# The last two gate blocks tile by tile, output weights in half rows, the output projection's first two token blocks together

## The chip, the cores and the metric

The kernel runs on one core of one Trainium2 chip. The metric is the device time of one execution in microseconds (us); the time of before is the median of three runs. The engines are named as in the profile: PE (TensorE, matmuls), PEld (its weight loads), DVE (VectorE), ACT (ScalarE), POOL (GpSimd) and SP (SyncE, which here issues all DMA transfers). "PSUM" is the memory that matmuls write, "bank" one of its [128, 512] float32 tiles.

## The reference, cut to what matters

One layer of a mixer over 2048 tokens of width 1024: a modulated norm, one input projection, four branches (RG-LRU, short convolution, Fourier, SSD), each gated, and one output projection of their 4 x 512 = 2048 columns.

```python
y_rg, rg_st = rglru(rg_x, lp, rg_h0, True)
y_ssd, ssd_st = ssd_branch(ssd_xbc, ssd_dt, ssd_z, lp, ssd_h0, True)
y_sc = shortconv_branch(sc_b, sc_c, sc_x, lp, rows)
y_fn = fourier_branch(fn_x)
ycat = jnp.concatenate([y_rg * jax.nn.silu(rg_g), y_sc * jax.nn.silu(sc_g),
                        y_fn * jax.nn.silu(fn_g), y_ssd], axis=-1)
return ycat.astype(h.dtype) @ lp['w_out'], rg_st, ssd_st
...
x = x + gate * out
...
return rmsnorm(x, final_norm_w)
```

## The kernel before

Every product is made of three matmuls, since an operand is kept as a high part and a rest (`split`, L210: ACT copies the high part, L139, and DVE or POOL subtracts it, L214): high by high, high by rest, rest by high. One tile of an input projection (`proj`, L229) is 8 steps of 128 rows, so 24 matmuls of 128x128 by 128x512 (L142 to L144). A block of weights (`wload`, L219) covers 128 columns; its halves come through one buffer `wraw`, and the block lies in one of two slots, `whi`/`wlo` 0 and 1, which a block frees with its last matmul.

The stages stand in the source in this order: modulation, RG-LRU, z and dt, SSD inputs, Fourier mixing, the SSD's first chunks, short convolution and RG-LRU gates, the last gate (`fngate`, four blocks of 128 columns, each over four tiles of 512 tokens), and the output projection over 16 blocks of 128 tokens. The tile framework's scheduler settles the order of each engine's instructions from its own model of times before the program runs; on the chip each queue then runs in that order, so an instruction that waits holds all behind it.

The SSD goes by 16 chunks of 128 tokens. `ssd_head` (L965) makes scores (PE L982, masked on DVE L986), the next state (L678), two products with the entering state (PE L1004, L1005, from `hs` that DVE makes in L1002), and the decayed scores `ma` (DVE L1022, L1027, L1032, L1033, with ACT and POOL). `ssd_tail` (L1037) multiplies them (L1044), gates, norms (the last step is DVE L1057), transposes (PE L1060), and stores the result by a DMA to `ycat`. `ssd_chunk(c)` is the head of chunk c+1 and the tail of chunk c. `NEARLY` chunks stand ahead of the gates; the others stand in the output projection's loop, chunk b + `NEARLY` ahead of block b.

The output projection of a token block takes four quarters of its 2048 rows (`oproj`, L1148), in the order of the branches: quarter 3 is the SSD's. A quarter is loaded from `ycat` (`oyr`), split (`ysplit`, to `oyhl`), and multiplied with the two halves of 512 columns: 24 matmuls (L1153 to L1155) into two banks, `ps_mm` and `ps_tr`. Of either there are two buffers. The 16 weight rows-of-128 are loaded in the last gate block as [128, 1024] tiles (`wo_raw`: two buffers and a weight slot that is not in use), split, and put where the tokens' columns `h_hi`, `h_lo` of a 512-token tile have been read for the last time: quarter q takes the places of tile q. The first token block's projection (`op0`) directly follows the last gate, since the gates' weight slots give it its buffers.

Of the kernel before, what the change touches and what calls it, by code (L numbers as in the profile page):

```python
# [8 lines left out]
F32 = mybir.dt.float32  # L9
# [24 lines left out]
def constants():  # L34
# [5 lines left out]
    # channel transform: [cos 0..64 | sin 0..63], with the ortho norm and the gate's half  # L40
# [6 lines left out]
    # token transform: rows in blocks (window of 256, parity)  # L47
# [10 lines left out]
    # [par*4+w][cos/sin][128][f] -> split f into two tiles  # L58
# [11 lines left out]
def layout(x, c, ctx, c_ctx, ada_w, ada_b, norm_w, w_in, w_out, rg_conv_w, rg_conv_b, rg_gate_a_w, rg_gate_a_b,  # L70
# [7 lines left out]
    # [block of columns k][row within 128][rows / 128][shift | scale]  # L78
# [43 lines left out]
def build(tc, A, out):  # L122
# [23 lines left out]
    def softplus(pl, x, n, dst, scale_in=1.0, tag=None, bufs=None):  # L146
        """dst = log(1 + exp(scale_in * x)) for a [128, n] tile, exact also where it is small."""
# [27 lines left out]
    def mbank(four):  # L175
        """a bank for a projection; with four, of those of the transposes too"""
        nbank[0] += 1
        return bank("tr" if four and nbank[0] % 2 else "mm")
# [7 lines left out]
    # ---------------------------------------------------------------- constants  # L186
# [20 lines left out]
    # ---------------------------------------------------------------- weight blocks  # L207
# [3 lines left out]
    def split(hi, lo, raw, eng):  # L211
        """raw (float32) as a high part and a rest, both of 12 bits"""
        copy_hi(hi, raw)
        eng.tensor_tensor(lo, raw, f32(hi), SUB)  # L214
# [20 lines left out]
    # ---------------------------------------------------------------- adaLN shift and scale  # L235
# [10 lines left out]
    def norm_rows(xt):  # L246
        """scales the rows of xt [128, 1024] by 1/rms"""
# [8 lines left out]
    # high and low part of the four columns side by side: one pass over the matrix' high part serves both  # L256
# [7 lines left out]
    # [k][:, who] = shift, norm_w * (1 + scale)  # L264
# [31 lines left out]
    # ---------------------------------------------------------------- normed, modulated, transposed tokens  # L296
# [30 lines left out]
    def conv_silu(pl, b, projs, n, emit, nb=3):  # L327
        """causal-ish convolution of 4 taps and silu over consecutive tiles of n tokens, each then given to emit"""
# [48 lines left out]
    # ---------------------------------------------------------------- first columns: RG-LRU input, context  # L377
# [30 lines left out]
    # the first tile of tokens and three blocks of weights run along with the columns of the modulation's matrix  # L408
# [35 lines left out]
    # dt of the context, by columns  # L444
# [45 lines left out]
    # ---------------------------------------------------------------- RG-LRU  # L490
# [788 lines left out]
```

## Time and profile before

| | |
|---|---|
| median of three runs | 1653.36 us (1651.04 to 1655.83) |
| span of the profiled execution | 1656.3 us |
| mean granted TensorE clock | 0.980 |
| busy: PE, DVE, ACT, POOL | 1569.4, 1053.3, 714.9, 564.3 us |
| gate blocks 2 and 3 | 1149.0 to 1202.5 us of the span |
| output projection | from 1202.5 us on |
| its regular period for one token block | 27.4 us |

The profiled execution has no other time than its span; it lies 2.9 us above the median and 0.5 us above the highest of the three runs. The share of busy time says which engine has the most work; where time is lost is told by the idle times in front of PE's instructions, each with the engine that ended it. A shown duration of a matmul is longer than the distance to the next one, since matmuls are pipelined: distances of starts tell the rate.

### The profile page before, as it was taken

What the parts mean: (1) busy time and instruction counts of PE and PEld (TensorE: products, weight loads), DVE (VectorE), ACT (ScalarE), POOL (GpSimd) and SP (SyncE); (2) the same over time, 40 slices, a digit from 0 to 9 for tenths busy, and PEclk for the clock granted to TensorE, in tenths of its full rate; (3) what the DMA queues carried; (4) which work ended last, traced back from release to release, by engine and by line L of the source; (5) the groups of instructions that cost most, each with busy time, mean ns of one, the idle gap of its engine ahead of it and who ended that gap; (6) DMA issues with size and microseconds to landing.
All of it is one profiled execution on the core that took longest, in us unless ns stands there. A gap on an engine that the chain in (4) does not pass through costs nothing. (4 is left out here: it accounts for less than half of the span.)

```text
span 1656.3 us, 22749 instructions
## 1 busy us (share of the span) xinstructions
PE 1569.4 (95%) x7906; PEld 1271.5 (77%) x7906; DVE 1053.3 (64%) x1837; ACT 714.9 (43%) x1383; POOL 564.3 (34%) x536
## 2 busy tenths in 40 slices
PE   6899999899899999899999999898988999999998
PEld 3687899777788778666788888785766777777787
DVE  7765354698986657644168653437468777878653
ACT  5654046557465536211222324424345544545432
POOL 5533123312211422343315345334423424243310
PEclk9999999999999999999999999999999999999999
DMA  8424232323332231454222236657575655555532
GB/s 328 153 87 135 87 99 92 106 90 104 124 116 71 83 121 58 148 156 128 77 79 61 87 109 179 174 161 233 165 254 171 183 146 171 146 170 148 162 105 70
DMA packets 182257, 220.93 MB, mean 133 GB/s; under 512 B 20183, under 2 KB 118905, under 8 KB 182142
## 3 DMA queue, kind: packets, MB, share of 16 engines
q1 hardware_dynamic: 182142, 219.48, 42.8%
q8 instruction: 62, 1.02, 0.3%
q14 instruction: 53, 0.43, 0.1%
HBM read 155.40 MB, written 64.03 MB: 132 GB/s over the span
## 5 line engine op out<-in xcount | busy, mean ns | idle before, releaser
L142 PE MATMUL ps_mm<-h_hi,whi 128*128 128x512 f32 x696 | 276.9, 401 | 5.6 <-ACT craw L347 4.5
L143 PE MATMUL ps_mm<-h_lo,whi 128*128 128x512 f32 x696 | 278.7, 400 | 1.8 <-DVE h_lo L309 1.0
L144 PE MATMUL ps_mm<-h_hi,wlo 128*128 128x512 f32 x696 | 278.3, 400 | 0.0
L142 PEld LDWEIGHTS ps_mm<-h_hi,whi 128*128 128x128 f32 x696 | 133.1, 192 | 36.2 <-ACT craw L347 5.4
L143 PEld LDWEIGHTS ps_mm<-h_lo,whi 128*128 128x128 f32 x696 | 133.3, 192 | 31.6 <-DVE h_lo L309 2.2
L144 PEld LDWEIGHTS ps_mm<-h_hi,wlo 128*128 128x128 f32 x696 | 133.6, 192 | 28.9 <-issue 1.4
L142 PE MATMUL ps_tr<-h_hi,whi 128*128 128x512 f32 x384 | 151.6, 395 | 0.0
L143 PE MATMUL ps_tr<-h_lo,whi 128*128 128x512 f32 x384 | 151.5, 395 | 0.0
L144 PE MATMUL ps_tr<-h_hi,wlo 128*128 128x512 f32 x384 | 151.1, 394 | 0.0
L1153 PE MATMUL ps_mm<-wo_hi,oyhl 128*128 128x512 f32 (+1 forms) x272 | 106.9, 393 | 7.5 <-ACT oyhl L139 7.5
L139 ACT ACTIVATE whi<-wraw 128x512 fp32r<-128x512 f32 (+1 forms) x77 | 49.6, 645 | 143.4 <-DMA wraw<-wblk 98.4
L1155 PE MATMUL ps_mm<-wo_hi,oyhl 128*128 128x512 f32 (+1 forms) x272 | 106.2, 391 | 2.8 <-DVE oyhl L214 2.7
L1154 PE MATMUL ps_mm<-wo_lo,oyhl 128*128 128x512 f32 (+1 forms) x272 | 106.9, 393 | 0.0
L1009 POOL TENSOR_TENSOR y<-y,e 128x256 f32<-128x256 f32 x32 | 35.6, 1114 | 195.3 <-DVE e L1008 195.3
L1154 PE MATMUL ps_tr<-wo_lo,oyhl 128*128 128x512 f32 (+1 forms) x256 | 100.4, 392 | 0.0
L1155 PE MATMUL ps_tr<-wo_hi,oyhl 128*128 128x512 f32 (+1 forms) x256 | 100.0, 390 | 0.0
L1153 PE MATMUL ps_tr<-wo_hi,oyhl 128*128 128x512 f32 (+1 forms) x256 | 99.1, 387 | 0.0
L214 POOL TENSOR_TENSOR wlo<-wraw,whi 128x512 fp32r<-128x512 f32 (+1 forms) x40 | 61.7, 1543 | 97.3 <-ACT whi L139 81.8
L142 PEld LDWEIGHTS ps_tr<-h_hi,whi 128*128 128x128 f32 x384 | 72.8, 190 | 16.8 <-issue 2.1
L143 PEld LDWEIGHTS ps_tr<-h_lo,whi 128*128 128x128 f32 x384 | 72.6, 189 | 16.4 <-issue 1.7
L144 PEld LDWEIGHTS ps_tr<-h_hi,wlo 128*128 128x128 f32 x384 | 72.6, 189 | 15.6 <-issue 1.1
L139 ACT ACTIVATE oyhl<-oyr 128x512 fp32r<-128x512 f32 x68 | 42.6, 627 | 96.2 <-PE ps_tr L1155 72.6
(365 smaller groups left out, 3847.9 us busy)
## 6 DMA issues: line engine op xcount, KB each, us to landing
wraw<-wblk SPq DMA_DIRECT2D x74, 256.0 KB, 3.0
oyr<-ycat SPq DMA_DIRECT2D x68, 256.0 KB, 3.4
ci<-cst_d SPq DMA_DIRECT2D x64, 256.0 KB, 3.5
xs<-xsb_d SPq DMA_DIRECT2D x31, 320.0 KB, 3.0
adar<-ada SPq DMA_DIRECT2D x16, 512.0 KB, 10.2
hf_d<-r_v SPq DMA_DIRECT2D x32, 256.0 KB, 2.2
ycat<-gy SPq DMA_DIRECT2D x32, 256.0 KB, 2.4
wo_raw<-wout SPq DMA_DIRECT2D x16, 512.0 KB
```

The source lines that it names most:

```text
L139: act.activation(dst, src, AF.Copy)
L142: pe.matmul(ps, wh, xh, start=start, stop=False)
L143: pe.matmul(ps, wh, xl, start=False, stop=False)
L144: pe.matmul(ps, wl, xh, start=False, stop=stop)
L214: eng.tensor_tensor(lo, raw, f32(hi), SUB)
L1009: pool.tensor_tensor(y[:, s], y[:, s], e[:, 0:256], ADD)
L1153: pe.matmul(p, yhl[:, 0, j], wo_hi[q][:, j, c0:c1], start=first and j == 0, stop=False)
L1154: pe.matmul(p, yhl[:, 0, j], wo_lo[q][:, j, c0:c1], start=False, stop=False)
L1155: pe.matmul(p, yhl[:, 1, j], wo_hi[q][:, j, c0:c1], start=False, stop=last and j == 3)
```

## The change

One more SSD chunk (head of chunk 2, tail of chunk 1) stands ahead of the gates and no longer in the loop. Gate blocks 2 and 3 both get their weights first, and their tiles go by turns: tile 0 of block 2, tile 0 of block 3, tile 1 of block 2, and so on. The output weights come as 32 half rows of [128, 512] through four buffers. The first two token blocks of the output projection run quarter by quarter side by side, on all four banks of `ps_mm` and `ps_tr`: quarters 0 and 1 with buffers in the weight slots, quarters 2 and 3 with those of the loop.

```diff
-    NEARLY = 1
+    NEARLY = 2
...
-        for j in range(3):
+        for j in range(2):
             w = wload(B_FNG + j)
             for tt in range(4):
                 fngate(w, j, tt)
-        w = wload(B_FNG + 3)
+
+        ws = [wload(B_FNG + j) for j in (2, 3)]
         free = wcount[0] % 2
         for tt in range(4):
-            fngate(w, 3, tt)
+            for j in range(2):
+                fngate(ws[j], 2 + j, tt)
...
-                if (4 * tt + j) % 3 < 2:
-                    r = qr.tile([128, 1024], F32, name="wo_raw", tag="wo_raw", bufs=2)
-                else:
-                    r = wp.tile([128, 1024], F32, name="wo_raw", tag=f"wlo{free}")
-                ld(r, A["wout"][4 * tt + j])
...
+                for c0 in (0, 512):
+                    cs = slice(c0, c0 + 512)
+                    r = qr.tile([128, 512], F32, name="wo_raw", tag="wo_raw", bufs=4)
+                    ld(r, A["wout"][4 * tt + j][:, cs])
...
-        op0 = [bank("mm"), bank("tr")]
-        for q in range(4):
-            yr = wp.tile([128, 4, 128], F32, name="oyr", tag="wraw", bufs=1)
-            yhl = wp.tile([128, 2, 4, 128], F32R, name="oyhl",
-                          tag=(f"whi{free}", f"whi{1 - free}", f"wlo{1 - free}", f"whi{free}")[q])
-            ysplit(0, q, yr, yhl)
-            oproj(yhl, q, op0, halves, q == 0, q == 3)
+
+        op0 = [[bank("mm"), bank("tr")] for _ in range(2)]
+        for q in range(2):
+            for b in range(2):
+                yr = wp.tile([128, 4, 128], F32, name="oyr", tag="wraw", bufs=1)
+                yhl = wp.tile([128, 2, 4, 128], F32R, name="oyhl", tag=f"{('whi', 'wlo')[b]}{(free + q) % 2}")
+                ysplit(b, q, yr, yhl)
+                oproj(yhl, q, op0[b], halves, q == 0, False)
...
+    qye = ExitStack()
+    qy = qye.enter_context(pool_of("qy", right))
+    for q in range(2, 4):
+        for b in range(2):
+            oproj(yhl_of(b, q), q, op0[b], halves, False, q == 3)
...
-                op_ = op0 if b == 0 else [bank("mm"), bank("tr")]
-                for q in range(4 if b else 0):
+                op_ = op0[b] if b < 2 else [bank("mm"), bank("tr")]
+                for q in range(4 if b >= 2 else 0):
```

What it does to the queues is seen at three places. The first is PE's queue at the end of gate block 2's first tile (`ps_tr_10486` before; `h_hi1` is token tile 1). Before, with what each instruction waits for:

```order
L144 MATMUL ps_tr_10486<-h_hi0_246,wlo_10475 128x512
L1060 MATMUL ps_bb_7660<-ident_66,y_7469 128x128 [waits DVE_49]
L1060 MATMUL ps_bb_7660<-ident_66,y_7469 128x128 x3
L142 MATMUL ps_mm_10518<-h_hi1_856,whi_10474 128x512
L143 MATMUL ps_mm_10518<-h_lo1_857,whi_10474 128x512
```

And after the change, where `whi_10613`, `wlo_10614` are block 3's weights and `whi_10603` block 2's:

```order
L144 MATMUL ps_tr_10625<-h_hi0_246,wlo_10604 128x512
L142 MATMUL ps_mm_10657<-h_hi0_246,whi_10613 128x512 [waits Activation_49]
L143 MATMUL ps_mm_10657<-h_lo0_247,whi_10613 128x512
L142 MATMUL ps_tr_10723<-h_hi1_856,whi_10603 128x512
L144 MATMUL ps_mm_10657<-h_hi0_246,wlo_10614 128x512 [waits Pool_49]
```

Block 3's first tile, with its weights, moved ahead of block 2's second tile; chunk 0's transposes (L1060) and chunk 2's head now stand behind it.

The second place is PE's queue at the first quarter 3 that has to wait for a chunk of its own. Before, that is in token block 1 (`wo_hi_10754` is quarter 2's weights, `wo_hi_10804` quarter 3's); this is the end of the stretch between chunk 1's transposes and quarter 3:

```order
L678 MATMUL ps_ba<-xw,xs 64x256 x2
L1154 MATMUL ps_mm<-wo_lo_10755,oyhl 128x512
L1155 MATMUL ps_mm<-wo_hi_10754,oyhl 128x512
L1153 MATMUL ps_tr<-wo_hi_10754,oyhl 128x512
L1004 MATMUL ps_ba<-hs,ch 128x512
L1005 MATMUL ps_ba<-hs,cl 128x512
L1154 MATMUL ps_tr<-wo_lo_10755,oyhl 128x512
L1155 MATMUL ps_tr<-wo_hi_10754,oyhl 128x512
L1153 MATMUL ps_mm<-wo_hi_10804,oyhl 128x512
```

After, in token block 2 (`wo_hi_10883` is quarter 2, `wo_hi_10981` quarter 3), from chunk 2's transposes on:

```order
L1060 MATMUL ps_bb<-ident,y 128x128 x4
L1044 MATMUL ps_bb<-xs,ma 128x64
L982 MATMUL ps_ba<-cct,bt 128x128
L1044 MATMUL ps_bb<-xs,ma 128x64 x6
L678 MATMUL ps_ba<-xw,xs 64x256 x2
L1044 MATMUL ps_bb<-xs,ma 128x64
L1155 MATMUL ps_mm<-wo_hi_10883,oyhl 128x512
L1153 MATMUL ps_tr<-wo_hi_10883,oyhl 128x512
L1154 MATMUL ps_tr<-wo_lo_10884,oyhl 128x512
L1155 MATMUL ps_tr<-wo_hi_10883,oyhl 128x512
L1004 MATMUL ps_ba<-hs,ch 128x512
L1153 MATMUL ps_mm<-wo_hi_10981,oyhl 128x512
```

The place moved by one token block, and four of quarter 2's matmuls lie between where sixteen lay.

The third is the SP queue at the end of the output weights. Before, with the first block's quarters 2 and 3 (`oyr_10882`, `oyr_10911`):

```order
L134 DMA oyr_10882<-ycat0_147 128x4x128
L134 DMA wo_raw_10768<-wout 128x1024
L134 DMA ycat3_150<-gy_10772 128x512
L134 DMA wo_raw_10806<-wout 128x1024
L134 DMA oyr_10911<-ycat0_147 128x4x128
L134 DMA wo_raw_10810<-wout 128x1024
L134 DMA wo_raw_10814<-wout 128x1024
L134 DMA wo_raw_10818<-wout 128x1024
```

After (`oyr_11048` and `oyr_11077` are the second block's quarter 0 and the first block's quarter 1, `oyr_11106` the second block's quarter 1):

```order
L134 DMA oyr_11048<-ycat0_147 128x4x128
L134 DMA wo_raw_10987<-wout 128x512
L134 DMA wo_raw_10991<-wout 128x512
L134 DMA wo_raw_10995<-wout 128x512
L134 DMA ycat3_150<-gy_10917 128x512
L134 DMA oyr_11077<-ycat0_147 128x4x128
L134 DMA wo_raw_10999<-wout 128x512
L134 DMA ycat3_150<-gy_10949 128x512
L134 DMA wo_raw_11003<-wout 128x512
L134 DMA wo_raw_11007<-wout 128x512
L134 DMA wo_raw_11011<-wout 128x512
L134 DMA oyr_11106<-ycat0_147 128x4x128
```

Of a token block's quarters, 2 and 3 stood among the last weights' loads; now no quarter beyond 1 does, and the second block's quarter 1 follows the last weight.

## Rows read from the trace of the kernel before

**Rows 1.** The page's first part: busy time, share of the span, instructions

```profile
PE 1569.4 (95%) x7906; PEld 1271.5 (77%) x7906; DVE 1053.3 (64%) x1837; ACT 714.9 (43%) x1383; POOL 564.3 (34%) x536
```

**Rows 2.** Waits of PE from 900 us on: total us, times, longest

```profile
PE ps_mm L1153 <- ACT oyhl L139: 7.5, 2, 6.2
PE ps_ba L982 <- DMA cct<-ct_d: 3.9, 1, 3.9
PE ps_ba L1004 <- DVE gm L986: 3.4, 2, 2.1
PE ps_mm L1155 <- DVE oyhl L214: 2.7, 2, 1.4
PE ps_ba L1004 <- DVE hs L1002: 2.4, 2, 2.2
```

**Rows 3.** Stretches: sum, busy PE, PEld, DVE, ACT, POOL, clock, DMA share, GB/s

```profile
1140.00:1160.00 20.00, 17.03 (x78) 12.20 (x77) 19.21 (x38) 9.84 (x28) 10.69 (x10) 1.00 0.70 209
1160.00:1180.00 20.00, 17.83 (x70) 13.97 (x69) 13.10 (x22) 7.86 (x17) 12.39 (x11) 0.91 0.47 150
...
1329.00:1356.40 27.40, 27.40 (x129) 21.21 (x128) 20.64 (x47) 13.40 (x33) 9.81 (x9) 1.00 0.54 156
```

**Rows 4.** Timeline of PE, gate blocks 2 and 3: start, duration, instruction, idle before

```profile
1149.02 0.39 PE L142 MATMUL ps_tr<-h_hi,whi 128*128 128x512 f32 x1
...
1154.10 0.47 PE L1004 MATMUL ps_ba<-hs,ch 128*128 128x512 f32 x1 [2.08 <-DVE gm L986]
...
1165.71 0.51 PE L1004 MATMUL ps_ba<-hs,ch 128*128 128x512 f32 x1 [2.17 <-DVE hs L1002]
...
1167.00 0.63 PE L142 MATMUL ps_mm<-h_hi,whi 128*128 128x512 f32 x1
1167.42 0.63 PE L143 MATMUL ps_mm<-h_lo,whi 128*128 128x512 f32 x1
...
1180.75 0.39 PE L142 MATMUL ps_tr<-h_hi,whi 128*128 128x512 f32 x1
```

**Rows 5.** Timeline of PE, output projection's first token block

```profile
1202.51 0.39 PE L1153 MATMUL ps_mm<-wo_hi,oyhl 128*128 128x512 f32 x1
...
1209.37 0.50 PE L1153 MATMUL ps_mm<-wo_hi,oyhl 128*128 128x512 f32 x1 [1.25 <-ACT oyhl L139]
...
1211.53 0.80 PE L1155 MATMUL ps_mm<-wo_hi,oyhl 128*128 128x512 f32 x1 [1.44 <-DVE oyhl L214]
...
1219.94 0.50 PE L1155 MATMUL ps_mm<-wo_hi,oyhl 128*128 128x512 f32 x1 [1.28 <-DVE oyhl L214]
...
1226.96 0.49 PE L982 MATMUL ps_ba<-cct,bt 64*128 64x128 f32 x2
```

**Rows 6.** The tile wo_raw: instructions, durations in ns, first and last start

```profile
L1187 DVE SCALAR_TENSOR_TENSOR wo_lo<-wo_raw,cols,wo_hi x4: 1283/1284/1286, 1222.1 to 1229.0; 128x1024 fp32r<-128x1024 f32 x4
```

**Rows 7.** Timeline of PE from chunk 1's transposes to quarter 3

```profile
1250.73 0.60 PE L1060 MATMUL ps_bb<-ident,y 128*128 128x128 f32 x4
...
1258.61 0.40 PE L1155 MATMUL ps_tr<-wo_hi,oyhl 128*128 128x512 f32 x1
1265.22 0.79 PE L1153 MATMUL ps_mm<-wo_hi,oyhl 128*128 128x512 f32 x1 [6.21 <-ACT oyhl L139]
```

**Rows 8.** Timeline of the SP queue in that stretch

```profile
1254.10 0.39 SPq L134 DMA_DIRECT2D ycat<-yt  x1
...
1258.18 0.43 SPq L134 DMA_DIRECT2D oyr<-ycat  x1
```

**Rows 9.** Timeline of ACT there

```profile
1264.54 0.63 ACT L139 ACTIVATE oyhl<-oyr 128x512 fp32r<-128x512 f32 x1 [5.18 <-DMA oyr<-ycat]
```

**Rows 10.** Timeline of DVE: the last part of gate block 3's weights

```profile
1165.69 0.69 DVE L214 TENSOR_TENSOR wlo<-wraw,whi 128x512 fp32r<-128x512 f32 x1
```

**Rows 11.** DVE by line and form, 1137 to 1167 us: busy us, mean ns

```profile
L1022 DVE TENSOR_SCALAR ci<-ci,pk 128x128 f32<-128x128 f32 x16 | 6.2, 438 | 0.2 <-DMA ci<-cst_d 0.2
L1033 DVE TENSOR_TENSOR ma<-ma,ci 128x512 f32<-128x512 f32 x3 | 3.8, 1277 | 0.0
```

**Rows 12.** The same from 1329 to 1356.4 us

```profile
L1022 DVE TENSOR_SCALAR ci<-ci,pk 128x128 f32<-128x128 f32 x8 | 1.7, 278 | 3.5 <-DMA ci<-cst_d 3.5
L1033 DVE TENSOR_TENSOR ma<-ma,ci 128x512 f32<-128x512 f32 x2 | 1.4, 680 | 0.0
```

More of the change, by code (lines that the diff above doesn't have):

```diff
@@ L1169, in build @@
                 fngate(w, j, tt)
-        w = wload(B_FNG + 3)
+        ws = [wload(B_FNG + j) for j in (2, 3)]
         free = wcount[0] % 2
         for tt in range(4):
-            fngate(w, 3, tt)
+            for j in range(2):
+                fngate(ws[j], 2 + j, tt)
             hi, lo = H16(f"wo_hi{tt}", 2 * tt, F32R, (4, 1024)), H16(f"wo_lo{tt}", 2 * tt + 1, F32R, (4, 1024))
             for j in range(4):
-                if (4 * tt + j) % 3 < 2:
-                    r = qr.tile([128, 1024], F32, name="wo_raw", tag="wo_raw", bufs=2)
-                else:
-                    r = wp.tile([128, 1024], F32, name="wo_raw", tag=f"wlo{free}")
-                ld(r, A["wout"][4 * tt + j])
-                if tt < 3:
-                    split(hi[:, j], lo[:, j], r, pool if j == 2 else dve)
-                else:
-                    nw = cols[:, C_SNW + j:C_SNW + j + 1]
-                    act.activation(hi[:, j], r, AF.Copy, scale=nw)
-                    dve.scalar_tensor_tensor(lo[:, j], r, nw, f32(hi[:, j]), MUL, SUB)
+                for c0 in (0, 512):
+                    cs = slice(c0, c0 + 512)
+                    r = qr.tile([128, 512], F32, name="wo_raw", tag="wo_raw", bufs=4)
+                    ld(r, A["wout"][4 * tt + j][:, cs])
+                    if tt < 3:
+                        split(hi[:, j, cs], lo[:, j, cs], r, pool if j == 2 else dve)
+                    else:
+                        nw = cols[:, C_SNW + j:C_SNW + j + 1]
+                        act.activation(hi[:, j, cs], r, AF.Copy, scale=nw)
+                        dve.scalar_tensor_tensor(lo[:, j, cs], r, nw, f32(hi[:, j, cs]), MUL, SUB)
@@ new lines, in build, with yhl_of @@
+        for q in range(2):
[4 more added lines that the diff above has]
+                oproj(yhl, q, op0[b], halves, q == 0, False)
+    def yhl_of(b, q):
+        yr = qy.tile([128, 4, 128], F32, name="oyr", tag="oyr", bufs=3)
+        yhl = qy.tile([128, 2, 4, 128], F32R, name="oyhl", tag="oyhl", bufs=2)
+        ysplit(b, q, yr, yhl)
+        return yhl
@@ L1197, in build @@
+    qye = ExitStack()
[3 more added lines that the diff above has]
+            oproj(yhl_of(b, q), q, op0[b], halves, False, q == 3)
     wpe.close()
-    with pool_of("qy", right) as qy, pool_of("q6", left) as q6:
+    with pool_of("q6", left) as q6:
         fnw = q6.tile([128, 1024], F32, name="fnw")
@@ L1204, in build @@
         ld(gate_b, gate_d.partition_broadcast(128))
-        def yhl_of(b, q):
-            yr = qy.tile([128, 4, 128], F32, name="oyr", tag="oyr", bufs=3)
-            yhl = qy.tile([128, 2, 4, 128], F32R, name="oyhl", tag="oyhl", bufs=2)
-            ysplit(b, q, yr, yhl)
-            return yhl
         def residual(p, xr, c0, c1, ss):
@@ L1261, in build @@
                 st(o_[:, 0:512], xr[:, 0:512])
+    qye.close()
     sdp.close()
```

## The prediction

> **What bounds the kernel now.** I read the page's busy times first, then PE's waits, then the timeline of PE around each of them. PE is busy for 95% of the span [rows 1]; DVE, next, for 64%. In the regular part of the output projection, from 1329 us on, PE is busy for the whole of each stretch of 27.4 us [rows 3], and the list of PE's waits [rows 2] has nothing that falls later than 1300 us. So PE's own work is the floor there, and an edit pays only where PE stands idle or runs at a lower rate. The change leaves the number of matmuls as it is and moves them, between about 1149 and 1300 us. The reader should see in [rows 2] which waits lie there: two on ScalarE's part of `oyhl` (7.5 us, 6.2 of it in one), two on VectorE's part (2.7), two on `gm` (3.4, the longer 2.1), two on `hs` (2.4, one of 2.2).
>
> The full rate is read where nothing waits: from 1180.75 [rows 4] to 1202.51 us [rows 5] lie four tiles of 24 matmuls, 21.76 us or 0.2267 us a matmul, 5.44 us a tile or quarter. Behind some waits the distance is 0.42 us (1167.00 to 1167.42 [rows 4]): that is the lower of TensorE's two clock levels, 1.2 instead of 2.4 GHz, and it follows a wait of 2.17 us in these rows. The granted clock of 1160 to 1180 us is 0.91 [rows 3].
>
> **Part 1: the first token blocks side by side, weights in half rows.** Before, 80 matmuls of the first block run from 1202.51 to 1226.96 us [rows 5], 24.45 us, where 80 x 0.2267 = 18.1 would do: 6.3 us are lost, 1.25 + 1.44 + 1.28 us as waits on `oyhl`, the rest as matmuls held up within their queue or at the lower level. With T for the projection's start at 1202.51, quarter 1 was needed at T + 5.4 and whole at T + 9.0 (1211.53); quarter 2 was needed at T + 10.9 and waited for until T + 17.4 (1219.94). Side by side, a quarter lasts for two blocks, 10.9 us, so quarter 1 is needed at T + 10.9 and quarter 2 at T + 21.8: both later than they were ready before. The last weights were split until 1229.0 + 1.3 = T + 27.8 [rows 6]; quarter 3 is now needed at T + 32.7. The second block's data are loaded in addition, one after another through one buffer in the weight slots, at most 5 us for load and split (5.4 us of PE's work covers each). The change also lets weights start sooner, since a token tile is read for the last time two tiles ahead of the next one, 10.9 us instead of 5.4. The 32 loads instead of 16 cost SP 16 more issues of some 0.4 us (as the loads of [rows 8]), in the cover of 43.5 us of matmuls. Thus the 6.3 us go, bounded by 3.3 (one load lands three us late) and 6.3. I take **-6.3**.
>
> **Part 2: the wait on `gm`.** Chunk 2's head no longer follows on the first block's projection; what stands there is chunk 3's head, with 19 matmuls, 4.3 us, between its scores and its first use of `hs`. The second wait on `gm`, 3.4 - 2.1 = 1.3 us [rows 2], is covered: **-1.3**, bounds -1.3 and 0.
>
> **Part 3: the wait of 6.2 us moves, it does not go.** Before, chunk 1's transposes are at 1250.73 us, the branch's result is stored from 1254.10 us [rows 8], the reload as a quarter is issued at 1258.18, lands some six us later, is split at 1264.54 [rows 9], and quarter 3 begins at 1265.22 us: a chain of 14.5 us, of which PE's own work covers 8.3, up to 1259.0 (the last matmul starts at 1258.61 [rows 7]). After the change blocks 0 and 1 have their chunks early. But in block 2 the transposes of chunk 2 stand right in front of quarter 3 again, with only 16 small matmuls of the chunk, two of its state, two of its entering state and four of quarter 2 between, about 4.8 us. Here the queue's order decides, not the time at which the data could be there. The chain could be as short as 10.0 us (the store 3.8 us and the load 3.4 us of the same tiles, and some 2.8 for ACT, the issues and the split) or as long as before: a wait of 5.2 to 9.7 us. I take 6.2 as before, nearer to the lower end, since the SP queue has less in it there than at 1254 us: **0**, bounds -1.0 and +3.5. Behind a wait as long as this the lower level follows in both kernels.
>
> **Part 4: the gate stretch.** The two blocks ran from 1149.02 to 1202.51 us, 53.5 us for 192 matmuls (43.5) and 2.7 us of chunk work: 7.3 us lost, of them 2.08 and 2.17 as waits on `gm` and `hs` [rows 4]. After the change two things differ. First, block 3's first tile needs its weights at once. They come no sooner, since they take the slot of block 1, whose last matmul is at 1149.02 us: the last part of them was made by VectorE at 1165.69 + 0.69 = 1166.4 us [rows 10], 17.4 us behind. In this time PE did 41 matmuls and some chunk work before; the new order gives it all of block 2's tile 0 and most of block 3's, and by counting rows up to the weights' last part PE is ahead of before by about **-1.4**. Secondly, chunk 2's head and chunk 1's tail come into the stretch. Their matmuls are only moved. Their VectorE work is not free: VectorE was busy for 19.21 of 20 us from 1140 us, and for 13.10 of the next 20 [rows 3]. From the weights' last part to the `hs` of chunk 2's second half it now has about 18.9 us of work if its operations last as in the regular part [rows 12], and 24.1 at the prices of this stretch (1277 ns instead of 680 for L1033, 438 instead of 278 for L1022 [rows 11]), while PE's queue has 16.1 us in between. PE waits 2.8 us by the one and 8.0 by the other, or not at all if VectorE gets ahead as in the idle third that it had behind 1160 us. I take **+2.8**, since POOL's tensor work, which stands beside the dear rows, is less behind 1166 us, and +0.7 for the lower level behind one wait in two: 3.5, bounds 0 and 11.
>
> The dear prices in [rows 11] are those of VectorE's operations with POOL at work for 10.7 of 20 us [rows 3]. The Trainium skill, "SBUF — State Buffer", section "SBUF: two separate sides", says that VectorE and GpSimd share a pair of SBUF ports, which one of them holds for a whole instruction while the other waits; it speaks against packing one more chunk among POOL's gate products, and by it the dear end holds as long as POOL is at work. The two row groups agree with it (1277 against 680 ns).
>
> **The sum** against the profiled execution: -6.3 - 1.3 + 0 - 1.4 + 3.5 = -5.5 us of 1656.3. The profiled run lies 2.9 us above the median, and the difference is the same for either: 1653.4 - 5.5 = 1647.9. A part of the loss before that I didn't price is 3.9 us on `cct` [rows 2], ahead of the change, which may come a few tenths sooner; I say 1648. Forecast alone: 1643 to 1653.
>
> **The rivals.** (A) The gate stretch takes back what the projection gives. It is the price of a chunk among the gates: the two blocks lose 7.3 us with one chunk among them; if the further chunk costs as much there, the 3.5 - 1.4 of part 4 become +7.3, and the sum is -6.3 - 1.3 + 7.3 = -0.3: 1653.1, no change. For it: VectorE at 19.21 of 20 us [rows 3]. Against: it has a third free behind 1160 us. (B) Slower: VectorE stays at the dear prices to the end of the gate blocks. Then chunk 2's `hs` comes 8.0 us late, 3 us more go at the lower level behind it, and the chain of part 3 takes its full 14.5 us (+3.5): -6.3 - 1.3 + 3.5 + 8.0 + 3.0 = +6.9, and without the -1.4 of part 4: 1660. It passes the time of before once the gates lose more than some 6 us beyond what they lose now. For it: rows 11; against: POOL's share there is not all tensor work that collides, and the regular part does as much per chunk at the lower prices. (C) Quarter 3 of block 2 doesn't wait: its chain ends within the cover, because chunk 2's result could be there long before. Then part 3 is -6.2 - 1.2 for the lower level behind it, instead of 0: the sum is -12.9, 1640.5. Against: chain and cover hang on one queue's order, and 10.0 us of chain do not fit in 4.8. (D) The tiles by turns might wait for weights throughout, so that the change doesn't do what it says: but only the first of block 3's tiles comes near to 1166.4 us, the others follow by 10.9 us, so this is inside the bounds of part 4.
>
> **How the numbers follow.** Forecast 0.53, A 0.25, B 0.12, C 0.10. The likeliest is the forecast, **1648**. A measurement of this kernel tells about 0.3% from no change, 5 us: faster means under 1648.4. The forecast's own range lies on both sides of this mark; of its 0.53 I give 0.36 to faster, since most of its bounds and the unpriced `cct` lie on that side, and 0.17 to no change. With C that is 0.46 for faster; A and the rest of the forecast make 0.42 for no change. B gives 0.12 for slower. For a range of 8 in 10 I leave out B's far half and the ends of C: 1640 to 1657.
>
> **What would show it.** In the profile after: the waits of L1153 and L1155 on `oyhl` shrink to one of 5 to 10 us, in token block 2, behind L1060; blocks 0 and 1 run 192 matmuls in 43.5 us without a gap; no wait on `gm` behind the projection's start; in the gate stretch a wait on weights or on `hs` of up to 8 us, and VectorE close to full from 1166 us on. Wrong would be: gaps among the 192 matmuls (part 1), VectorE's L1033 near 1.3 us up to the projection (then A or B), or no wait at block 2's quarter 3 (then C).

## The result

The changed kernel takes 1665.8 us (median of five runs, 1663.1 to 1670.1) against 1653.4 us (1648.3 to 1657.2): a ratio of 1.0075, 95% interval 1.0053 to 1.0097, so 12 us slower where 1648 was forecast. It also lies outside the range (1640 to 1657).

The page's first line of times, to be held against [rows 1], shows that no work was added to PE, and 11 us to VectorE:

```profile
PE 1569.2 (94%) x7906; PEld 1270.3 (76%) x7906; DVE 1064.7 (64%) x1850; ACT 714.7 (43%) x1399; POOL 558.9 (34%) x539
```

PE's waits of the changed kernel from 900 us on (in all, times, longest; before: [rows 2]):

```profile
PE ps_mm L1153 <- ACT oyhl L139: 11.2, 2, 7.0
PE ps_ba L982 <- DMA cct<-ct_d: 5.2, 1, 5.2
PE ps_ba L1004 <- DVE hs L1002: 4.4, 3, 2.5
PE ps_ba L1004 <- DVE gm L986: 3.8, 3, 1.6
PE ps_mm L1155 <- DVE oyhl L214: 3.2, 4, 1.7
```

The kinds of waits are the same; the one on ScalarE's part of `oyhl` has two long ones now. The timeline of PE (start, duration, instruction, idle time before it) says where; the second line is the last matmul of the gates, the next the first of the output projection, to be held against [rows 5] and [rows 7]:

```profile
1200.36 0.39 PE L142 MATMUL ps_mm<-h_hi,whi 128*128 128x512 f32 x1
...
1205.57 0.39 PE L144 MATMUL ps_mm<-h_hi,wlo 128*128 128x512 f32 x1
...
1212.93 0.80 PE L1153 MATMUL ps_mm<-wo_hi,oyhl 128*128 128x512 f32 x1 [6.97 <-ACT oyhl L139]
...
1280.52 0.60 PE L1060 MATMUL ps_bb<-ident,y 128*128 128x128 f32 x4
...
1289.96 0.50 PE L1153 MATMUL ps_mm<-wo_hi,oyhl 128*128 128x512 f32 x1 [4.20 <-ACT oyhl L139]
...
1424.52 0.50 PE L1155 MATMUL ps_mm<-wo_hi,oyhl 128*128 128x512 f32 x1 [1.67 <-DVE oyhl L214]
...
1428.90 0.49 PE L1004 MATMUL ps_ba<-hs,ch 128*128 128x512 f32 x1 [1.59 <-DVE gm L986]
```

The wait of 4.2 us at 1289.96 is the one that the prediction placed in block 2. That of 7 us at the projection's very first matmul, and those behind 1305 us, it did not have.

**Where the time went.** To add up small losses too, I took from each trace the distance of each PE instruction to the next and subtracted what its form takes where nothing waits: 0.2268 us for a matmul of 128x512, and for the chunk's forms 0.113 (L1044), 0.108 (L1060), 0.145 (L678), 0.36 (L1004), 0.425 (L1005), 0.207 (L982). The sums, in us, start 26 us ahead of chunk 1's first scores (L982), so that differences of the first 1110 us between executions are left out. "Gates" ends with the gates' last matmul; the token blocks are numbered as in the code, from 0. The rows below **after** are the experiments, which the next section explains one by one. Each ratio is against runs of before on the same chip.

| kernel | median us | ratio to before, 95% | gates | start, blocks 0 and 1 | block 2 | 3 to 7 | rest | sum |
|---|---|---|---|---|---|---|---|---|
| before | 1653.4 | 1 | 15.8 | 17.0 | 0.9 | 2.2 | 2.7 | 38.6 |
| before_again | 1654.8 | 0.9998 (0.9985 to 1.0011) | 17.7 | 15.8 | 0.9 | 2.2 | 3.1 | 39.8 |
| **after** | 1665.8 | 1.0075 (1.0053 to 1.0097) | 17.5 | 10.6 | 5.8 | **13.6** | 3.0 | 50.5 |
| lead_one | 1656.8 | 1.0024 (1.0014 to 1.0034) | 18.7 | 11.9 | 6.3 | 4.3 | 3.2 | 44.4 |
| near_two | 1655.6 | 1.0014 (1.0004 to 1.0025) | 21.2 | 9.1 | 2.4 | 2.6 | 2.5 | 37.9 |
| one_block | 1658.0 | 1.0035 (1.0020 to 1.0049) | 18.5 | 18.3 | 0.4 | 2.0 | 2.7 | 41.9 |
| no_turns | 1674.0 | 1.0119 (1.0101 to 1.0137) | 19.4 | 16.7 | 8.4 | 14.3 | 3.0 | 61.7 |
| no_turns_lead | 1669.0 | 1.0082 (1.0066 to 1.0098) | 18.0 | 14.4 | 8.6 | 7.3 | 2.9 | 51.2 |
| lead_one_rows | **1650.7** | **0.9976** (0.9966 to 0.9987) | 19.0 | 10.0 | 0.8 | 2.2 | 3.2 | 35.2 |
| lead_one_six | 1655.4 | 1.0007 (0.9998 to 1.0017) | 21.7 | 3.9 | 6.9 | 3.0 | 3.2 | 38.7 |
| lead_one_less | 1657.9 | 1.0018 (1.0009 to 1.0028) | 21.8 | 11.8 | 5.5 | 2.4 | 3.0 | 44.5 |
| turns_halves | 1653.6 | 0.9994 (0.9985 to 1.0004) | 17.0 | 15.8 | 0.4 | 1.7 | 3.2 | 38.1 |
| turns_rows | 1668.9 | 1.0081 (1.0067 to 1.0095) | 16.6 | 27.0 | 0.8 | 5.5 | 3.0 | 53.0 |
| halves_only | 1666.6 | 1.0075 (1.0062 to 1.0087) | 15.3 | 29.6 | 0.8 | 2.2 | 3.2 | 51.1 |
| rows_first_split | 1659.1 | 1.0027 (1.0017 to 1.0036) | 21.0 | 11.5 | 5.0 | 2.3 | 2.9 | 42.7 |
| first_own | 1664.7 | 1.0064 (1.0046 to 1.0082) | 17.6 | 15.3 | 6.5 | 2.5 | 2.6 | 44.5 |
| rows_first_pool | 1664.7 | 1.0056 (1.0043 to 1.0068) | 21.0 | 8.1 | 4.3 | 10.4 | 3.0 | 46.7 |

For the change: 50.5 - 38.6 = 11.9 us, as the ratio has it (0.0075 x 1653.4 = 12.4). The gates give +1.7, the start with the first three blocks 16.4 instead of 17.9 (-1.5), and blocks 3 to 7 give +11.4. The spans of the two profiled executions, 1664.0 and 1656.3 us, differ by only 7.7 us: in every other execution that has both numbers the time is 1.7 to 1.9 us above the span, so the profiled execution of before took about 1658 us, some 4.7 above its median and not 2.9. A column is one profiled execution, good to one or two us (before against before_again), so that of these three differences only the +11.4 is clear of the noise; with first_own the profiled execution was 6.6 us shorter than the median, so its sum says little, and of its trace only the waits are used.

### The profile page after: what moved, and what is told of

Its sections match the earlier page's. It is cut to its first block, busy times and chain, and to the rows that moved or that the text cites. A ratio compares the mean times of both kernels' runs of the same rounds, so it can differ in the third digit from the quotient of the medians.

```text
span 1664.0 us, 22814 instructions
## 1 busy us (share of the span) xinstructions
PE 1569.2 (94%) x7906; PEld 1270.3 (76%) x7906; DVE 1064.7 (64%) x1850; ACT 714.7 (43%) x1399; POOL 558.9 (34%) x539
## 5 line engine op out<-in xcount | busy, mean ns | idle before, releaser
L214 POOL TENSOR_TENSOR wlo<-wraw,whi 128x512 fp32r<-128x512 f32 (+1 forms) x40 | 61.7, 1542 | 101.0 <-ACT whi L139 85.5
L142 PEld LDWEIGHTS ps_tr<-h_hi,whi 128*128 128x128 f32 x384 | 72.5, 189 | 16.6 <-issue 2.1
L143 PEld LDWEIGHTS ps_tr<-h_lo,whi 128*128 128x128 f32 x384 | 72.4, 189 | 16.7 <-issue 2.3
L144 PEld LDWEIGHTS ps_tr<-h_hi,wlo 128*128 128x128 f32 x384 | 72.7, 189 | 15.8 <-issue 1.3
L214 DVE TENSOR_TENSOR oyhl<-oyr,oyhl 128x512 fp32r<-128x512 f32 x68 | 49.7, 730 | 49.3 <-ACT oyhl L139 49.1
```

Source lines behind the costliest of these rows:

```text
L142: pe.matmul(ps, wh, xh, start=start, stop=False)
L143: pe.matmul(ps, wh, xl, start=False, stop=False)
L144: pe.matmul(ps, wl, xh, start=False, stop=stop)
```

## The experiments

**The late losses.** From 1305 us on, where before had no wait at all, PE of the changed kernel waits often and briefly (PE's waits from 1305 to 1452 us):

```profile
PE ps_mm L1155 <- DVE oyhl L214: 2.6, 2, 1.7
PE ps_ba L1004 <- DVE gm L986: 2.4, 2, 1.6
PE ps_ba L1004 <- DVE hs L1002: 0.4, 1, 0.4
PE ps_bb L1060 <- DVE y L1057: 0.3, 1, 0.3
PE ps_ba L678 <- issue: 0.2, 1, 0.2
```

All but 0.2 us of it is on VectorE. The waits add up to 5.9 of the 13.6 us; the rest, of which before has 2.2 too, is matmuls held up in PE's queue or run at the lower clock level. Two stretches there (length, busy time of PE, PEld, DVE, ACT, POOL, granted clock, DMA share, GB/s; before: the last of [rows 3]):

```profile
1332.00:1359.00 27.00, 26.06 (x118) 18.89 (x116) 25.46 (x59) 13.26 (x34) 9.95 (x10) 1.00 0.59 186
...
1413.00:1440.00 27.00, 23.75 (x101) 17.68 (x101) 19.32 (x43) 12.30 (x32) 8.12 (x9) 0.94 0.46 133
```

In the first, VectorE is busy for 25.46 of 27 us, where a regular period needs 20.64 of 27.4; it is the fullest of the five such stretches from 1305 to 1440 us. Its operations are hardly slower than in [rows 12] (VectorE by line and form, 1332 to 1359 us: busy us, mean ns):

```profile
L1022 DVE TENSOR_SCALAR ci<-ci,pk 128x128 f32<-128x128 f32 x12 | 2.9, 304 | 0.7 <-DMA ci<-cst_d 0.7
L1033 DVE TENSOR_TENSOR ma<-ma,ci 128x512 f32<-128x512 f32 x3 | 2.1, 687 | 0.0
```

It does more of them, because chunks come faster. The second stretch has PE's two longest late waits, and there VectorE is not full: 19.32 of 27 us. Timelines of SP's queue and of VectorE ahead of the wait at 1424.52:

```profile
1419.14 0.32 SPq L134 DMA_DIRECT2D ci<-cst_d  x1
```

```profile
1423.18 0.68 DVE L1022 TENSOR_SCALAR ci<-ci,pk 128x128 f32<-128x128 f32 x3 [4.08 <-DMA ci<-cst_d]
1423.78 0.68 DVE L214 TENSOR_TENSOR oyhl<-oyr,oyhl 128x512 fp32r<-128x512 f32 x1
```

The split that PE waits for (last line) stands behind L1022, and VectorE is idle for 4.08 us in front of that, until a load of a chunk's `ci` lands. The masks `gm` that PE waits for at 1398.28 us (0.80 us) stand behind such an idle time too, of 1.81 us; in front of the wait of 0.94 us at 1339.34 us VectorE runs without a pause. So PE waits in two ways: VectorE has too much to do, or it waits for a chunk's own load with PE's next operand behind it.

The transposes that end a chunk (timeline of PE) come at

```profile
1302.28 0.49 PE L1060 MATMUL ps_bb<-ident,y 128*128 128x128 f32 x3
...
1322.07 0.60 PE L1060 MATMUL ps_bb<-ident,y 128*128 128x128 f32 x4
...
1347.63 0.55 PE L1060 MATMUL ps_bb<-ident,y 128*128 128x128 f32 x3
...
1369.47 0.66 PE L1060 MATMUL ps_bb<-ident,y 128*128 128x128 f32 x4
```

that is 67.2 us for three chunks, 22.4 us each instead of 27.4. Counting matmuls between, the first three chunks' transposes are through when 2.71 blocks have been multiplied, a lead of 0.29 (chunks through less blocks multiplied); eleven are through at 8.61 blocks, a lead of 2.39. Before, the lead in the regular part is 1.39 (six chunks at 4.61 blocks). The source explains it: the loop calls for chunk b + `NEARLY` ahead of block b, and `NEARLY` is now 2. The side-by-side blocks use up the lead that the extra chunk had given, and the loop then asks for more lead than before. That is theory L. The experiment takes the second part away:

```diff
-            if b + NEARLY < 16:
-                ssd_chunk(b + NEARLY)
+            if 2 <= b + 1 < 16:
+                ssd_chunk(b + 1)
```

> The changed kernel, but the loop of the output projection asks for chunk b + 1 ahead of block b (as before the change) instead of chunk b + 2; the two chunks ahead of the gates stay. Compared with the changed kernel (1665.8). Theory L (late gain lost to a catch-up: side by side, two blocks are projected before chunk 2's result, and the loop then asks for a lead of two chunks, so VectorE has to do two chunks too many between 1280 and 1440 us): PE's losses behind the third block fall from about 16 us to 5 to 8, time 1655 to 1659. Rival R (the extra losses there come from the two blocks side by side, whatever lead is asked for): no change, 1664 to 1668. The wait of 7 us at the projection's start stays under both.

Measured 1656.8 us, and the losses of blocks 3 to 7 fall from 13.6 to 4.3. PE's waits in the same stretch:

```profile
PE ps_mm L1155 <- DVE oyhl L214: 0.4, 1, 0.4
PE ps_ba L1004 <- DVE hs L1002: 0.4, 1, 0.4
PE ps_ba L1004 <- DVE gm L986: 0.2, 1, 0.2
```

L stands, R falls for this order. Is the lead of two dear by itself? Where the blocks don't run side by side, less has to be made up: with one more chunk early as the only edit the lead is 1.42 when three chunks are through, so 1.0 chunk is missing to 2.39, not 2.1.

```diff
-    NEARLY = 1
+    NEARLY = 2
```

> The kernel before, with one more chunk ahead of the gates as the only edit (loop asks for chunk b + 2). Theory L: no catch-up is needed, since chunk 1's result is there before block 0, so the wait of 6.2 us at block 1's quarter 3 goes or shrinks to block 2 and behind it PE loses little: 1644 to 1652. Rival G (the extra chunk among the gates costs as much as the others there, and a lead of two chunks is dear by itself): 1656 to 1664.

near_two is the kernel before with this line alone. It measured 1655.6 us, between the two theories and close to G: blocks 3 to 7 lose only 2.6 (L was right), the start and the first blocks 9.1 instead of 17.0, but the gates 21.2 instead of 15.8 (17.7 in before_again), as G said. So rival A of the prediction (the gates take back what the projection gives) is what an extra chunk alone does.

```diff
-        op0 = [[bank("mm"), bank("tr")] for _ in range(2)]
+        op0 = [[bank("mm"), bank("tr")]]
...
-            for b in range(2):
+            for b in range(1):
```

> The changed kernel with only the first token block ahead of the loop, so that nothing runs side by side; the extra chunk, the tiles by turns and the half rows stay. Theory L: no catch-up behind the third block (losses there under 6 us), but the waits at the projection's start stay or grow, since a quarter lasts 5.4 us again: 1652 to 1662. Rival R agrees on the first part; rival G expects 1662 or more.

one_block (the same for quarters 2 and 3 and in the loop) measured 1658.0 us, with 2.0 us lost in blocks 3 to 7: with lead two and no side by side there is hardly a catch-up (a lead of 2.00 when three chunks are through). The second test of L is in another order of the gates, with blocks 2 and 3 one after the other (no_turns) and with the loop's lead of one besides (no_turns_lead):

```diff
-        for j in range(2):
+        for j in range(3):
...
-        ws = [wload(B_FNG + j) for j in (2, 3)]
+        w = wload(B_FNG + 3)
...
-            for j in range(2):
-                fngate(ws[j], 2 + j, tt)
+            fngate(w, 3, tt)
```

> The changed kernel with gate blocks 2 and 3 one after the other again; the extra chunk, half rows and two blocks side by side stay. Theory W (the wait of 7 us on the first quarter's split comes from the weights in half rows, whose four buffers hold 8 KB a partition instead of 12 with the free slot, and whose splits stand ahead of it in ScalarE's queue): the wait stays or grows to 7 to 14 us, time 1664 to 1672. Rival T (it comes from the tiles by turns): the wait goes, 1656 to 1660.

> no_turns (1674.0: two blocks side by side, half rows, gate blocks one after the other) with the loop's chunks one ahead instead of two. Theory L: the losses between the third and the ninth block, 14 us in no_turns, fall to 2 to 6, time 1663 to 1668. Rival: the late losses belong to this order of weights, time over 1670.

1674.0 and 1669.0 us; blocks 3 to 7 lose 14.3 and 7.3. The direction is that of L; the fall is 7.0 us, after 9.3 in lead_one, and what is left and the time lie just outside what L expected. In all traces, held against the regular lead (1.39 or 2.39), the two kernels that have 2.1 chunks to make up when three are through, after and no_turns, lose 13.6 and 14.3 us there. The others have 1.1 or less to make up and lose 1.7 to 4.3, but for rows_first_pool (10.4, with 1.0 to make up), no_turns_lead (7.3, with 1.1) and turns_rows (5.5, with 0.1). So the lead asked for is the main cause in the changed kernel, and not the only thing that can cost PE time there.

**The wait at the projection's start.** ScalarE's timeline ahead of it:

```profile
1201.99 0.63 ACT L139 ACTIVATE wo_hi<-wo_raw 128x512 fp32r<-128x512 f32 x1 [1.40 <-DMA wo_raw<-wout]
...
1204.55 0.63 ACT L139 ACTIVATE wo_hi<-wo_raw 128x512 fp32r<-128x512 f32 x1 [1.43 <-DMA wo_raw<-wout]
1205.86 1.30 ACT L139 ACTIVATE wo_hi<-wo_raw 128x512 fp32r<-128x512 f32 x2 [0.67 <-DMA wo_raw<-wout]
1208.06 0.63 ACT L139 ACTIVATE wo_hi<-wo_raw 128x512 fp32r<-128x512 f32 x1 [0.90 <-DMA wo_raw<-wout]
1210.79 0.63 ACT L139 ACTIVATE wo_hi<-wo_raw 128x512 fp32r<-128x512 f32 x1 [2.10 <-DMA wo_raw<-wout]
1211.72 0.63 ACT L139 ACTIVATE wo_hi<-wo_raw 128x512 fp32r<-128x512 f32 x1 [0.30 <-DMA wo_raw<-wout]
1212.26 0.61 ACT L139 ACTIVATE oyhl<-oyr 128x512 fp32r<-128x512 f32 x1
```

The first quarter's copy (last line) stands behind six copies, from 1204.55 us on, of weights that PE needs two quarters later, and five of those wait for their loads. Its own data and buffer are ready: the data were issued at 1162.65 us, and the buffer is gate block 2's weight slot, free since 1200.36 us. Before, the same slot was free four tiles, 21.8 us, ahead of the projection, since gate block 3 ran alone behind it, and the copy was made at 1180.72 us, ahead of all the weights' copies. The issue after the change (SP's queue) and the copy before (ScalarE):

```profile
1162.65 0.37 SPq L134 DMA_DIRECT2D oyr<-ycat  x1
```

```profile
1180.72 0.63 ACT L139 ACTIVATE oyhl<-oyr 128x512 fp32r<-128x512 f32 x1 [4.55 <-PE ps_mm L143]
```

That the tiles by turns are the condition of this wait is seen over all kernels, those that are told below with them:

| gate blocks 2 and 3 | kernels | PE's wait for the first quarter's split, us |
|---|---|---|
| one after the other | before, before_again, near_two, no_turns, no_turns_lead, halves_only | none |
| by turns, that quarter as in the change | after, lead_one, one_block, turns_halves | 7.0, 7.7, 8.0, 5.3 |
| the same, with other buffers or loads for the weights | turns_rows, lead_one_rows, lead_one_six, lead_one_less | 6.2, 5.4, 1.8, 5.4 |
| by turns, that quarter changed | rows_first_split, rows_first_pool, first_own | 1.4, none, none |

So no_turns answers its own question about the start: the wait goes, as rival T said. T's time was wrong nonetheless: other waits came in its place, one of 7.3 us in the second block's first quarter, for a bank of the gates' last tiles, and the late losses of 14.3 us stayed.

The loads in turn wait for buffers that VectorE gives back; the waits of ScalarE and of SP's queue from about 1190 to 1213 us:

```profile
ACT wo_hi L139 <- DMA wo_raw<-wout: 10.2, 8, 3.2
```

```profile
SPq L134 <- DVE wo_lo L214: 12.3, 8, 3.6
```

Theory W said that the raw weights have too little memory: four half rows, 8 KB a partition, instead of 12 KB (two whole rows and the slot that the tiles by turns now need). Three kernels on top of lead_one, the first:

```diff
-                for c0 in (0, 512):
-                    cs = slice(c0, c0 + 512)
-                    r = qr.tile([128, 512], F32, name="wo_raw", tag="wo_raw", bufs=4)
+                for c0 in (0,):
+                    cs = slice(c0, c0 + 1024)
+                    r = qr.tile([128, 1024], F32, name="wo_raw", tag="wo_raw", bufs=2)
```

> lead_one (1656.8, which waits 7.7 us for the first quarter's split) with the output weights in whole rows through two buffers: the same 8 KB a partition, 16 loads instead of 32. Theory W (what limits the weights is the memory that their raw data have, over the time from a load's issue to the release of its buffer): as late or later, the wait at the projection's start is 7 to 12 us, time 1656 to 1662. Rival H (the half rows themselves are dear: twice the loads, twice the splits): the wait shrinks below 4 us, 1650 to 1654.

1650.7 us, faster than before, and than lead_one by 6 us (8 by the two ratios, since the two ran on different chips); the wait is 5.4 us, and it is PE's only wait behind 1200 us:

```profile
PE ps_mm L1153 <- ACT oyhl L139: 5.4, 1, 5.4
```

H had the time, but neither theory had this: the start improved by 2.4 us only, and the gain is in block 2 (0.8 instead of 6.3), because in this order chunk 2's transposes stand at 2.00 blocks instead of 2.71, so quarter 3 no longer waits.

The second (its edit of the gate's buffers left out):

```diff
-                    r = qr.tile([128, 512], F32, name="wo_raw", tag="wo_raw", bufs=4)
+                    if tt < 2 and (2 * j + c0 // 512) % 6 == 5:
+                        r = wp.tile([128, 512], F32, name="wo_raw", tag="wraw", bufs=1)
+                    else:
+                        r = qr.tile([128, 512], F32, name="wo_raw", tag="wo_raw", bufs=5)
```

> lead_one with more memory for the raw weights: five half-row buffers, paid with one instead of two buffers for the last gate's tanh, and for the first two token tiles' weights the gates' raw buffer as a sixth. Theory W: the wait of 7.7 us on the first quarter's split falls to 0 to 4 us, time 1649 to 1654. Rival V (the splits are late because VectorE is full with the extra chunk): no change, 1655 to 1658.

1655.4 us. The wait fell from 7.7 to 1.8 us, as W said, but the gates lost 3 us more than lead_one's, and the time followed by 1 to 3 us only.

The third:

```diff
-                    r = qr.tile([128, 512], F32, name="wo_raw", tag="wo_raw", bufs=4)
-                    ld(r, A["wout"][4 * tt + j][:, cs])
+                    if c0 == 0:
+                        r = qr.tile([128, 512], F32, name="wo_raw", tag="wo_raw", bufs=4)
+                        ld(r, A["wout"][4 * tt + j][:, cs])
```

> lead_one with half of the output weights' loads left out: of each row only the first 512 columns are loaded, and both column halves are split from them, so that all splits and matmuls stay. Theory W: the weights are ready much sooner, the wait at the projection's start goes to under 2 us, 1647 to 1652. Rival V: the splits on VectorE still set the time, the wait stays over 5 us, 1654 to 1658.

1657.9 us: a wait of 5.4 us and another of 2.4 stayed, though no copy of weights waited for a load any more. In this order ScalarE stood in front of the SSD gate's `tz` for 5.1 us, with the weights' copies and the first quarter behind it. W as the whole cause falls.

Is it the extra chunk (theory E)? one_block without it keeps only turns and half rows:

```diff
-    NEARLY = 2
+    NEARLY = 1
```

> The changed kernel without the extra chunk and without the second block: tiles by turns and weights in half rows stay. Theory E (the wait of 7 to 8 us for the first quarter comes from the extra chunk, whose work on VectorE, ScalarE and SP stands among the weights'): the wait falls below 3 us, the wait at block 1's quarter 3 is back (6 us), time 1650 to 1655. Theory W (it comes from the weights' raw buffers or the half rows): the wait stays 5 to 9 us, 1657 to 1663.

turns_rows has lead_one_rows' whole rows besides:

> As turns_halves, but with whole rows through two buffers: of the change only the tiles by turns are left, which take the weight slot from the raw weights (8 KB a partition instead of 12). Theory E: as turns_halves, 1650 to 1655. If half rows are dear by themselves, 3 to 6 us faster than turns_halves. If 8 KB are too little, a wait over 5 us at the projection's start in both, 1657 to 1663.

And halves_only is the kernel before with this loop in the place of its whole rows:

```diff
+                for c0 in (0, 512):
+                    cs = slice(c0, c0 + 512)
+                    r = qr.tile([128, 512], F32, name="wo_raw", tag="wo_raw", bufs=4)
+                    ld(r, A["wout"][4 * tt + j][:, cs])
```

> The kernel before with half rows through four buffers (8 KB a partition, the weight slot not used) as the only edit. If half rows or 8 KB are dear: the projection's start loses 10 us or more instead of 6.3, 1657 to 1665. If neither is: within 3 us of before.

turns_halves measured 1653.6 us, no different from before, with a wait of 5.3 us at the start: E falls for the wait, although its time is the one that E gave. turns_rows measured 1668.9 and halves_only 1666.6. By its own expectation halves_only says that half rows or 8 KB are dear (12 us), and turns_halves, which has both, says that they are not; whole rows made lead_one faster by 6 us and turns_halves slower by 15. The 27.0 and 29.6 us that turns_rows and halves_only lose in the first blocks are for the most part waits for `hs`, `e` and `gm` from VectorE and for `oyhl` from ScalarE. So the half rows have no price that holds in every order. What differs with them is the order that the scheduler makes: chunk 2's transposes, for one, stand at 2.02 blocks before, 1.00 in halves_only, 1.79 in turns_halves and 1.67 in turns_rows. That the order alone makes the difference is not shown, since no run changed it by itself.

Then the place in the queue (theory Q). rows_first_split writes both blocks' first quarter between the last two gate tiles (`weights` is the loop over a tile's rows, `first_split` the load and `ysplit` of quarter 0):

```diff
...
+            fngate(ws[0], 2, tt)
+            if tt == 3:
+                for b in range(2):
+                    first_split(b)
+            fngate(ws[1], 3, tt)
+            if tt == 3:
+                weights(2)
+            if tt != 2:
+                weights(tt)
```

> lead_one_rows (1650.7) with the first quarter's load and split of both blocks written ahead of the weights of tile 2. If the scheduler moves them ahead, the wait of 5.4 us shrinks to 0 to 3 us and the time to 1645 to 1649; if the order follows its own model of times whatever the source says, nothing changes, 1649 to 1653.

1659.1 us. The wait at the start fell to 1.4 us, but waits of 1.5 and 3.3 us on the next quarters and of 3.2 us at block 2's quarter 3 took its place, and the time is 8 us longer than lead_one_rows'. rows_first_pool gives the first block's quarter 0 to GpSimd:

```diff
+                if q == 0 and b < 1:
+                    ld(yr, ycat[0][0:4, :, 128 * b:128 * b + 128].rearrange("b c t -> c b t"))
+                    pool.tensor_copy(yhl[:, 0], yr)
+                    pool.tensor_tensor(yhl[:, 1], yr, f32(yhl[:, 0]), SUB)
```

> lead_one_rows (1650.7, waits 5.4 us at the projection's start) with the first block's first quarter split by GpSimd instead of ScalarE and VectorE, ahead of the last weights in its queue. Theory Q: the wait falls below 2 us, and if nothing else moves the time to 1646 to 1649. Rival: the buffer or the load is what is late, whichever engine splits: 5 us stay, 1650 to 1653.

1664.7 us. No wait at the start, as Q said; 5.2 us on the second block's first quarter instead, at 1220.61 us, and late losses of 10.4. first_own gives that quarter a buffer of its own (and the raw weights three buffers, the gate's `tg` one; these two edits are left out here):

```diff
-                yhl = wp.tile([128, 2, 4, 128], F32R, name="oyhl", tag=f"{('whi', 'wlo')[b]}{(free + q) % 2}")
+                if q + b == 0:
+                    yhl = qr.tile([128, 2, 4, 128], F32R, name="oyhl", tag="first", bufs=1)
+                else:
+                    yhl = wp.tile([128, 2, 4, 128], F32R, name="oyhl", tag=f"{('whi', 'wlo')[b]}{(free + q) % 2}")
```

> lead_one (1656.8) with a buffer of its own for the first block's first quarter, free long before the last gate's end; it is paid with three instead of four half-row buffers and one instead of two for the last gate's tanh. Theory Q (with the tiles by turns the first quarter's buffer, block 2's weight slot, is free only one tile before the projection, so its split comes behind the weights in ScalarE's queue): the wait of 7.7 us at the projection's start goes to under 1 us, even though the weights have less memory; what comes later depends on the weights: 1650 to 1660. Theory W (late weights hold the start): with 6 KB the wait grows, 1660 or more.

1664.7 us. PE's timeline at the start:

```profile
1204.09 0.50 PE L1153 MATMUL ps_mm<-wo_hi,oyhl 128*128 128x512 f32 x1 [0.37 <-DVE tg L1085]
...
1212.11 0.77 PE L1153 MATMUL ps_tr<-wo_hi,oyhl 128*128 128x512 f32 x1 [2.28 <-DVE tg L1085]
...
1220.85 0.80 PE L1153 MATMUL ps_mm<-wo_hi,oyhl 128*128 128x512 f32 x1 [6.69 <-DVE tg L1085]
```

The wait on the first quarter is gone, as Q said, and the next one shows, which had been behind it: the second block needs the two banks that hold the gates' last two tiles, and VectorE empties them (`tg`, L1085) behind splits of the weights and of a later quarter. first_own has only one buffer for `tg`, but no_turns and no_turns_lead, with two, wait for the same `tg` (7.3 and 7.1 us; these waits are in PE's rows of these kernels). So the side by side start has a second condition, the four banks, besides the first quarter's place in the queue.

**before_again**, a second profile of the kernel before, is the scale for the table:

> The kernel before, unchanged, for a second profile of it: the losses of PE behind 1100 us should again be 37 to 40 us in all, 16 to 18 of them from the last gate's end to the end of the second token block, and under 6 behind the third.

39.8 us in all, 15.8 in the start and the first two blocks, 0.9 and 2.2 in the next ones, 5.3 in all behind the third: as expected, but for the 15.8, a little under the 16 to 18.

## Why the prediction was wrong

**Part 4, the gates: the size right, the mechanism not.** +2.1 was forecast (-1.4 and +3.5); the trace has +0.7 for the two blocks by turns (8.1 us lost instead of 7.4) and +1.7 with what precedes them, both within the noise of a column. The +3.5 was a wait of 2.8 us for the `hs` of chunk 2's second half, with 0.7 for the lower clock level behind it. PE did not wait there, and not for gate block 3's weights either. What it did wait for are chunk 1's two places, as before: 2.55 us on `hs` and 1.45 us on `gm` ([rows 4]: 2.17 and 2.08). So that the size came out is in part luck: of the outcomes that the prediction listed for that wait, the one that came was "not at all".

**Part 2, the wait on `gm`: right**; there is none around the projection's start.

**Part 3, quarter 3's wait moves to block 2: right in kind**, 4.2 us instead of the 6.2 taken, so -2.0 where the bounds were -1.0 and +3.5; its cover lies between 1280.52 and 1285.7 us, 5.2 us where 4.8 were counted, and its chain is 9.4 us, shorter than the 10.0 that were the lower bound.

**Part 1, -6.3: wrong.** The step that failed is the comparison of the quarters' times. It took quarters 1 and 2 and the weights, and gave quarter 0 no line, since it made no wait before. With the tiles by turns its buffer comes free only one tile ahead, so its split moves behind weights in ScalarE's queue, and PE waited 7.0 us for it, plus 0.5 for its rest and the lower clock level behind it. These make 10.3 of the 10.6 us that the changed kernel loses in the start and blocks 0 and 1, so what the prediction said of the later quarters and of the weights held: none of them made PE wait. What was forecast as -7.6 for parts 1 and 2, with part 3 unchanged, measured -1.5. What would have told it is the position of that one split among ScalarE's instructions.

**The missing part, +11.4 in blocks 3 to 7.** This is the larger failure: a term that was put at nothing. The prediction let the change end at about 1300 us and took the loop behind block 2 for the regular part of before, where PE's own work is the floor, since PE's work per block is unchanged. It didn't count what each block asks of VectorE: with lead two after two blocks without chunks, two chunks more fall into six blocks. The trace of before had the numbers: 20.64 of 27.4 us on VectorE per period [rows 3] leaves 6.8 us a period, and two chunks more want about 2 x 13.8 us (20.64 less a token block's four splits of 0.71, two multiplications of 0.70, two additions of 0.68 and one scaling of 1.28), 27.6 us in six periods with 41 free. It fits on average, so the sum alone would not have told the loss. It is not spread evenly (25.46 of 27 us in one stretch, 19.32 in another), and part of VectorE's free time is its waiting for a chunk's loads of `ci`; what PE needs next stands in VectorE's queue behind either. lead_one shows that the lead asked for costs most of the 11.4 us (9.3); how that divides between the two is open.

Of the rivals, A's time (no change) was that of near_two, not of the change. B had the right sign; its mechanism, VectorE slow to the end of the gates with PE waiting for it, did not occur. One stretch up to the gates' end shows PE without a pause (length, busy PE, PEld, DVE, ACT, POOL, clock, DMA share, GB/s):

```profile
1180.00:1205.60 25.60, 25.60 (x115) 20.80 (x114) 23.55 (x31) 14.22 (x28) 20.68 (x16) 1.00 0.75 240
```

VectorE's prices stayed dear only in part there: from 1166 to 1206 us L1022 took 500 ns, L1033 682. The kernel became slower by late chunks 100 us and more behind the gates.

## What to carry to other kernels

Moving matmuls of a bound engine together takes cover from what follows: count, for each block behind the move, what the second engine has to do in it and what it waits for, and check whether a look-ahead that was raised "to fill" must be made up there. When buffers change hands, find in each engine's queue the one instruction that feeds the first product behind the move, and what stands ahead of it. And where a scheduler orders the queues anew, the price of a change is not the sum of its parts' prices: here whole rows were worth 6 us in one neighbourhood and cost 15 in another, and the best version, 1650.7 us, was the change with the loop's lead of one and whole rows.

## What was not expected of the hardware, and what stays open

The lower clock level (matmuls 0.43 us apart) followed waits of 2.55 us (1161.17), 7.0 us and 4.2 us, and in before one of 2.17 (1165.71); behind 1.45 us (1151.44), and in before behind 2.08 (1154.10), there was none. A wait of 1.67 us (1424.52) was not followed by it, but the next one, of 1.59 us and 4.4 us later (1428.90), was.

Open is how the 7 us at the start divide between the queue's place, the loads' lateness and the `tg` of the last tiles: the experiments on it removed one of them and showed the next, and none removed all. Open is also why rows_first_pool, no_turns_lead and turns_rows lose 10.4, 7.3 and 5.5 us in blocks 3 to 7 with a lead of one.
